# A two-layer decoder trunk on one core: three float32r products for the attention scores, factors moved to ScalarE, weight cuts tied behind evacuations, maximum taken with the bias

## The chip, the cores and the metric

The kernel runs on one core of a Trainium2 chip. What counts is the device time of one execution in microseconds; the kernel before took 751.36 us in the median of three runs (750.59 to 751.94).

## The reference, cut to what matters

The input is 256 tokens of width 1024, all in float32. There are two layers. The first mixes tokens with a dilated attention: 16 heads of 64, each in three groups (undilated, every 4th and every 16th key), whose results are weighted by the softmax of their log-denominators. The second layer uses one causal attention whose scores get a bias from summed forget gates. Each layer ends in a SwiGLU block of inner width 2816.

```python
def dilated_mixer(h, w_in, w_out):
    proj = (h @ w_in).reshape(B, S, N_GROUPS, 3, N_HEADS, HEAD_DIM)
    ...                                  # q and k rotated, v; per group:
    o, lse = dilated_band_attention(q, k, v, dil, window // dil)
    ...
    wts = jax.nn.softmax(jnp.stack(lses, axis=0), axis=0)
    o = jnp.einsum('gbsh,gbshd->bshd', wts, jnp.stack(outs, axis=0))
    return o.reshape(B, S, ATTN_WIDTH) @ w_out

def forgetting_mixer(h, w_in, b_f, w_out):
    ...
    c = lax.cumsum(log_f, axis=1)
    s = jnp.einsum('bihd,bjhd->bhij', qi, k) * scale
    s = s + ci[..., None] - ck[:, :, None, :]
    s = jnp.where(key_pos[None, :] <= qpos[:, None], s, NEG_INF)
    p = jax.nn.softmax(s, axis=-1)
    return jnp.einsum('bhij,bjhd->bihd', p, vf)

for i in range(DEPTH):                   # h is the residual stream
    h = h + mixer(rmsnorm(h, norm[i]))
    h = h + swiglu(rmsnorm(h, ffn_norm[i]), ffn_w_gu[i], ffn_w_down[i])
return rmsnorm(h, final_norm)
```

## The kernel before

Every large product is made of three float32r matmuls. A float32 operand is cut in two by `split` (lines 71 to 82): ScalarE copies it to float32r (the high half, L74) and VectorE subtracts that from the original (the low half, L78). `mm3` (L194) then sums high by high (L197), high by low and low by high (L202). Weights come as pieces of 128 x 2048: `piece` (L85) issues two loads on SP's queue into a ring of five raw buffers and makes one cut for each; `weights` (L148) keeps two pieces ahead of the one in use and makes the cuts at once, or hands the low halves to a list or orders them behind a given instruction (`after`).

The projections of the first attention run in units (`a_units`): one for each quad of four heads (hq), group g and kind w (0 q, 1 k, 2 v), with 48 products of 256 columns for q and k. Each unit's result fills one of two PSUM banks "mm". `rotated` (L423) turns q and k on VectorE: a shuffle and a product with cosines read the bank (L433, L434), then a product with sines and a sum (L435, L436). In the fourth unit (i = 3) half of the projection is done ahead, inside the third unit, so that the factors `r_a` of the norm can be spread over the columns on the way (L563) and multiplied into cosines and sines (L569) before the rotation of the third unit reads its bank.

The scores of group 0 (`scores_a`, L450) are float32 matmuls over the 64 rows of one head: for a pair of heads and two query blocks four matmuls, of 128 and of 256 keys. `softmax_a` takes maxima (L488), exponentials (L283) and multiplies by the reciprocal of the sums: for the first pair of a quad on ScalarE (L497, not in the last quad), for the second on VectorE (L499). Transposes (L293) and products with v (L304) follow some units later; the list `due` holds what is to run after which unit.

The second attention has twelve units (`b_units`), the last nine in a loop (from L922). L939 copies q (times 0.125) and k from PSUM on ScalarE. `scores_b` makes the same float32 matmuls (L855); VectorE adds the bias (L861) and takes the negative maxima (L865), ScalarE the exponentials (L283). The scores of a quad's first pair run in the middle of the unit behind its k, those of the second at that unit's end or behind it. The low halves of the weights cut in units 3 and 5 wait in the list `behind`, and `release` lets them go behind the scan of the gates and behind the first scores' sums.

The order on each engine is made by a scheduler when the program is built: by the order in the code, with `first()` moving an instruction some 300 places ahead, and with `tc.issue_after(x)` fixing that an instruction is issued behind x. At run time each engine goes through its own queue in order.

Of the kernel before, what the change touches and what calls it, by code (L numbers as in the profile page):

```python
# [16 lines left out]
P = 128  # L17
D = 1024
S = 256
# [12 lines left out]
def trunk(ctx: ExitStack, tc: tile.TileContext, T, out):  # L32
# [38 lines left out]
    def split(pair, view, src, early=True, after=None):  # L71
        hi, lo = pair
        with first() if early else nullcontext():
            a = nc.scalar.activation(view(hi), src, AF.Copy)  # L74
# [7 lines left out]
            return a, low(after)  # L82


    def piece(key, todo=None):  # L85
# [6 lines left out]
        for c in range(2):  # L92
# [7 lines left out]
            cut = lambda after=None, raw=raw, view=view: split((wh, wl), view, raw, False, after)  # L100
# [4 lines left out]
        if key == GATED:  # L105
            cut = lambda after=None: split((wh, wl), lambda y: y[:, :, 256:], wf32, False, after)
            todo.append(cut)
# [40 lines left out]
    def weights(nm, i, after=None, ahead=AHEAD):  # L148

        upto = order.index((nm, i)) + ahead  # L150
        while state["next"] <= min(upto, len(order) - 1):
# [3 lines left out]
            for cut in cuts:  # L155
                cut(after)
# [266 lines left out]
    def rotated(o, g, w):  # L423


        if g == 0:
            q = hrow(f"qk{w}")[:, :512].rearrange("p (a b) -> p a b", a=2)
# [8 lines left out]
        nc.vector.tensor_tensor(q, q, tmp, op=ALU.add)  # L436
        return q, read

    def scores_a(quad, g, pr=None):
# [5 lines left out]
        if g == 0:  # L445

            scs = [psum("sc") for _ in range(2)]
            for qb in range(2):
                for h in range(2):
                    nc.tensor.matmul(scs[h][:, qb * P:qb * P + (qb + 1) * P], q[hr[h], pr, qb * P:(qb + 1) * P],  # L450
                                     k[hr[h], pr, :(qb + 1) * P], start=True, stop=True)
# [27 lines left out]
    def softmax_a(quad):  # L479
# [49 lines left out]
    for i, (hq, g, w) in enumerate(a_units):  # L529
# [19 lines left out]
        if w < 2:  # L549
# [4 lines left out]
            if i == 2:  # L554
                values_12(quad["v"], lead)

                wt = weights("a_in", 1)
# [12 lines left out]
            q, read = rotated(o, g, w)  # L570
            quad["fm"][g, w] = q
# [275 lines left out]
    def scores_b(hq, pr):  # L847
# [5 lines left out]
        for qb in range(2):  # L853
            for h in range(2):
                last = nc.tensor.matmul(scs[h][:, qb * P:qb * P + (qb + 1) * P], b[0][own[h], pr, qb * P:(qb + 1) * P],  # L855
                                        b[1][own[h], pr, :(qb + 1) * P], start=True, stop=True)
        for h in range(2):
            s = p_tile()
            with first():
                bias_h = b["bias", pr][:, h * 3 * P:(h + 1) * 3 * P]  # L860
                added = nc.vector.tensor_tensor(s[:, :3 * P], scs[h][:, :3 * P], bias_h, op=ALU.add)  # L861
            for qb in range(2):
                j = h * 2 + qb
                sv = s[:, qb * P:qb * P + (qb + 1) * P]
# [228 lines left out]
```

## Time and profile before

| | |
|---|---|
| Median of three runs | 751.36 us |
| The profiled execution | 752.26 us |
| Its span in the profile | 750.5 us |
| Granted TensorE clock | 0.997 |
| TensorE busy | 740.2 us |
| VectorE busy | 500.7 us |
| ScalarE busy | 373.7 us |
| GpSimd busy | 67.3 us |

The profile has one execution. Rows of groups show line, engine, operation, what is written from what, shape and count, then busy time and mean ns of one, then the idle time of the engine before them and what ended it. PE is TensorE's matmuls, PEld its weight loads, DVE VectorE, ACT ScalarE, POOL GpSimd, SP the queue that issues loads. In the timeline the first two numbers are start and length in us; neighbours of one line and operation are merged, with their count. In the chain of waits the first number is a start, the second how long that step holds the chain. Matmuls overlap, so the length of one (0.28 us for 256 columns) is more than the distance between two starts. The first attention lasts until about 250 us, the second layer's from about 450 to 555 us; the rest is SwiGLU.

### The profile page before, as it was taken

To read this page: it belongs to the slowest core of one execution; us is meant where nothing else is said; L and a number is where in the kernel's file an instruction comes from. 1 tells how busy PE (TensorE), PEld (TensorE's weight loads), DVE (VectorE), ACT (ScalarE), POOL (GpSimd) and SP (SyncE) were. 2 spreads that over 40 slices of the span, in tenths; PEclk is the share of its full clock that TensorE was granted. 3 is DMA by queue.
4 is the path that set the end of the run, shared out by engine and by line. 5 is a ranking of instruction groups with operands and counts; after the bars stand their busy time and mean duration, and the time that the engine had idled before them with its cause. 6 is when DMAs were issued, how large, how long until landed. Compare 5 with 4: busy or idle time off the path is not lost.

```text
span 750.5 us, 14329 instructions
## 1 busy us (share of the span) xinstructions
PE 740.2 (99%) x5916; PEld 680.1 (91%) x5916; DVE 500.7 (67%) x752; ACT 373.7 (50%) x617; POOL 67.3 (9%) x98
## 2 busy tenths in 40 slices
PE   9999999999999999999999999999999999999996
PEld 7998989999998789999999988989889999999995
DVE  6987978876879376554556365799867545456533
ACT  7635537437427365444445355467556444445521
POOL 0600004004004000000000004312000000000001
PEclk9999999999999999999999999999999999999998
DMA  9865544645646267656567543784537665656601
GB/s 332 302 195 170 169 142 156 210 142 169 198 133 200 88 225 242 204 179 205 181 198 250 169 129 127 268 252 155 166 95 235 217 205 179 199 193 213 210 1 56
DMA packets 39441, 138.07 MB, mean 184 GB/s; under 512 B 4528, under 2 KB 5840, under 8 KB 39376
## 3 DMA queue, kind: packets, MB, share of 16 engines
q1 hardware_dynamic: 39232, 137.01, 55.3%
q8 instruction: 46, 0.75, 0.4%
q14 instruction: 19, 0.16, 0.1%
q10 hardware_dynamic: 144, 0.15, 0.1%
HBM read 136.07 MB, written 1.07 MB: 183 GB/s over the span
## 4 chain that ended last, share of the span: by engine, by line
PE 93%; ACT 2%; DVE 2%; DMA 2%; issue 1%; SPq 0%; POOL 0%; POOLq 0%; DVEq 0%; ACTq 0%
PE ps_mm L202 32%; PE ps_mm L197 17%; PE ps_tr L202 9%; PE ps_sc L202 8%; PE ps_o L202 7%; PE ps_tr L197 5%; PE ps_sc L197 4%; PE ps_o L197 4%; PE ps_o L304 2%; PE ps_tr L293 1%; DMA otl<-in_lead 1%; PE ps_sc L450 1%; PE ps_sc L466 1%; PE ps_sc L855 1%; ACT wh L74 1%; DMA raw<-in_a_in 1%
## 5 line engine op out<-in xcount | busy, mean ns | idle before, releaser
L74 ACT ACTIVATE wh<-raw 128x1024 fp32r<-128x1024 f32 x236 | 243.0, 1054 | 247.5 <-PE ps_mm L202 85.8
L78 DVE TENSOR_TENSOR wl<-raw,wh 128x1024 fp32r<-128x1024 f32 x236 | 287.7, 1238 | 81.8 <-ACT wh L74 81.5
L197 PE MATMUL ps_mm<-xt,wh 128*128 128x256 f32 x816 | 228.2, 280 | 0.7 <-DVE qk L434 0.7
L202 PE MATMUL ps_mm<-xt,wl 128*128 128x256 f32 x816 | 226.3, 277 | 0.1
L202 PE MATMUL ps_mm<-xt,wh 128*128 128x256 f32 x816 | 226.2, 277 | 0.0
L197 PEld LDWEIGHTS ps_mm<-xt,wh 128*128 128x128 f32 x816 | 153.3, 188 | 4.4 <-issue 3.3
L202 PEld LDWEIGHTS ps_mm<-xt,wl 128*128 128x128 f32 x816 | 153.4, 188 | 0.5 <-DVE wl L78 0.5
L202 PEld LDWEIGHTS ps_mm<-xt,wh 128*128 128x128 f32 x816 | 153.7, 188 | 0.0
L202 PE MATMUL ps_tr<-xt,wl 128*128 128x256 f32 x304 | 83.9, 276 | 0.0
L202 PE MATMUL ps_tr<-xt,wh 128*128 128x256 f32 x304 | 83.9, 276 | 0.0
L197 PE MATMUL ps_tr<-xt,wh 128*128 128x256 f32 x304 | 83.7, 276 | 0.0
L692 DVE TENSOR_TENSOR sa<-ps_tr,sa 128x256 f32<-128x256 f32 x38 | 16.1, 424 | 74.1 <-PE ps_tr L202 74.0
L202 PEld LDWEIGHTS ps_tr<-xt,wl 128*128 128x128 f32 x304 | 57.1, 188 | 0.0
L202 PEld LDWEIGHTS ps_tr<-xt,wh 128*128 128x128 f32 x304 | 57.1, 188 | 0.0
L197 PEld LDWEIGHTS ps_tr<-xt,wh 128*128 128x128 f32 x304 | 56.9, 188 | 0.0
L279 POOL COPY v<-v 32x256 f32<-32x256 f32 x64 | 36.1, 563 | 180.3 <-ACT v L275 177.6
L197 PE MATMUL ps_mm<-wh,xt 128*128 128x512 f32 (+1 forms) x144 | 50.1, 348 | 0.0
L202 PE MATMUL ps_mm<-wl,xt 128*128 128x512 f32 (+1 forms) x149 | 49.3, 336 | 0.0
L202 PE MATMUL ps_mm<-wh,xt 128*128 128x512 f32 (+1 forms) x149 | 49.2, 335 | 0.0
L167 POOL TENSOR_SCALAR rs<-ssq 128x1 f32<-128x1 f32 x7 | 2.1, 307 | 425.2 <-ACT junk L176 425.2
L197 PE MATMUL ps_sc<-wh,ah 128*128 128x512 f32 x80 | 31.4, 392 | 0.0
L202 PE MATMUL ps_sc<-wl,ah 128*128 128x512 f32 (+1 forms) x82 | 31.3, 385 | 0.0
(224 smaller groups left out, 1112.9 us busy)
## 6 DMA issues: line engine op xcount, KB each, us to landing
raw<-in_gu SPq DMA_DIRECT2D x88, 512.0 KB, 4.8
raw<-in_a_in SPq DMA_DIRECT2D x68, 512.0 KB, 4.4
raw<-in_dn SPq DMA_DIRECT2D x44, 512.0 KB, 4.5
raw<-in_b_in SPq DMA_DIRECT2D x24, 512.0 KB, 5.0
raw<-in_a_out SPq DMA_DIRECT2D x8, 512.0 KB, 4.5
raw<-in_b_out SPq DMA_DIRECT2D x8, 512.0 KB, 4.9
bias<-sums SPq DMA_DIRECT2D x8, 384.0 KB, 6.3
grow<-in_norms SPq DMA_DIRECT2D x4, 512.0 KB, 5.4
```

The lines of the kernel that those rows point to most:

```text
L74: a = nc.scalar.activation(view(hi), src, AF.Copy)
L78: return nc.vector.tensor_tensor(view(lo), src, view(hi).bitcast(F32), op=ALU.subtract)
L167: nc.gpsimd.tensor_scalar(m, s, rest, None, op0=ALU.add)
L197: nc.tensor.matmul(o, sh, mh, start=start, stop=False)
L202: last = nc.tensor.matmul(o[:, u], s, m[:, u], start=False, stop=end and u.stop == n)
L279: nc.gpsimd.tensor_copy(v[1 + a % 2][n:n + 32, a // 2 * S:a // 2 * S + S], by_t[a * 32:a * 32 + 32, t, g])
L293: nc.tensor.transpose(tr[:, i * P:(i + 1) * P], b, ident)
L304: nc.tensor.matmul(o[h * HD:(h + 1) * HD], v[:, c:c + HD], w(h), start=start, stop=stop)
L450: nc.tensor.matmul(scs[h][:, qb * P:qb * P + (qb + 1) * P], q[hr[h], pr, qb * P:(qb + 1) * P], k[hr[h], pr, :(qb + 1) * P], start=True, st ...
L466: nc.tensor.matmul(sc[h][c, o:o + 64], q[hr[h], pq, qb * P + a * 32:qb * P + a * 32 + 32], k[hr[h], pq].rearrange("p (b n) -> p b n", b=2) ...
L692: nc.vector.tensor_tensor(a, u, sg, op=ALU.mult)
L855: last = nc.tensor.matmul(scs[h][:, qb * P:qb * P + (qb + 1) * P], b[0][own[h], pr, qb * P:(qb + 1) * P], b[1][own[h], pr, :(qb + 1) * P], ...
```

## The change

It has four parts.

- Scores of group 0 and of the second attention: q and k are cut into high and low halves, and each float32 matmul becomes three float32r matmuls (high by high, high by low, low by high), on the same 64 rows and with the same 128 or 256 columns. In the first attention the rotated sum now goes to a buffer "qr" (two for each of these units, from the ring of three) and `split` makes the halves. In the second, L939 writes the high half and a new VectorE instruction makes the low half straight from PSUM.
- First attention: in the first three quads the factors of the second pair are applied on ScalarE too.
- Ties: the second low half of the piece cut in unit 3 is issued behind the read of the bank in `rotated`; in the second attention's loop the cuts of weights are issued behind the previous unit's q or k (high half behind high half, low half behind low half).
- Second attention: sum with the bias and negative maximum become one VectorE instruction for each query block, which writes the negated sum; the exponential reads it with scale -1.

```diff
-    def split(pair, view, src, early=True, after=None):
+    def split(pair, view, src, early=True, after=None, hold=None):
         hi, lo = pair
         with first() if early else nullcontext():
-            a = nc.scalar.activation(view(hi), src, AF.Copy)
+            with behind_(hold and hold[0]):
+                a = nc.scalar.activation(view(hi), src, AF.Copy)
...
-            return a, low(after)
+            return a, low(after or hold and hold[1])
...
+    PRODUCTS = ((0, 0), (0, 1), (1, 0))
...
         if g == 0:
-            q = hrow(f"qk{w}")[:, :512].rearrange("p (a b) -> p a b", a=2)
+            pair = ap.tile([P, 2, 2, S], F32R, tag="h", name=f"qk{w}", bufs=4)
+            q = ap.tile([P, 2, S], F32, tag="qr", name="rc", bufs=3)
...
-        nc.vector.tensor_tensor(q, q, tmp, op=ALU.add)
+        if g == 0:
+            nc.vector.tensor_tensor(tmp, q, tmp, op=ALU.add)
+            q = pair[:, 0], pair[:, 1]
+            split(q, lambda y: y, tmp, False)
+        else:
+            nc.vector.tensor_tensor(q, q, tmp, op=ALU.add)
...
-                for h in range(2):
-                    nc.tensor.matmul(scs[h][:, qb * P:qb * P + (qb + 1) * P], q[hr[h], pr, qb * P:(qb + 1) * P],
-                                     k[hr[h], pr, :(qb + 1) * P], start=True, stop=True)
+                for i, (y, z) in enumerate(PRODUCTS):
+                    for h in range(2):
+                        nc.tensor.matmul(scs[h][:, qb * P:qb * P + (qb + 1) * P],
+                                         q[y][hr[h], pr, qb * P:(qb + 1) * P], k[z][hr[h], pr, :(qb + 1) * P],
+                                         start=i == 0, stop=i == 2)
...
-                    if pr == 0 and quad["hq"] < 3:
+                    if quad["hq"] < 3:
                         nc.scalar.activation(s, s, AF.Copy, scale=f)
...
-                wt = weights("a_in", 1)
+                second = []
+                wt = weights("a_in", 1, second)
+                second.pop(0)()
...
             q, read = rotated(o, g, w)
+            if i == 2:
+                second.pop()(read)
...
-            with first():
-                bias_h = b["bias", pr][:, h * 3 * P:(h + 1) * 3 * P]
-                added = nc.vector.tensor_tensor(s[:, :3 * P], scs[h][:, :3 * P], bias_h, op=ALU.add)
+            bias_h = b["bias", pr][:, h * 3 * P:(h + 1) * 3 * P]
             for qb in range(2):
-                j = h * 2 + qb
-                sv = s[:, qb * P:qb * P + (qb + 1) * P]
-                nc.vector.tensor_reduce(nm[:, j:j + 1], sv, axis=AX.X, op=ALU.max, negate=True)
-                exps(sv, nm, den, j)
+                j, u = h * 2 + qb, slice(qb * P, qb * P + (qb + 1) * P)
+                with first():
+                    added = nc.vector.tensor_tensor_reduce(s[:, u], scs[h][:, u], bias_h[:, u], -1.0, -NEG, ALU.add,
+                                                           ALU.min, nm[:, j:j + 1])
+                nc.scalar.activation(s[:, u], s[:, u], AF.Exp, bias=nm[:, j:j + 1], scale=-1.0,
+                                     accum_out=den[:, j:j + 1])
...
+    held = None
     for i, (hq, w) in enumerate(b_units):
...
-        wt = weights("b_in", hq * 3 + w, behind if i in (3, 5) else None)
+        wt = weights("b_in", hq * 3 + w, behind if i in (3, 5) else None, hold=held)
...
-            bq[hq][w] = ap.tile([P, 2, S], F32, tag=f"fm{w}", name=f"fb{w}", bufs=2)
+            if w == 0:
+                low = ap.tile([P, 2, 2, S], F32R, tag="h", name="fl", bufs=4)
+            ov = o.rearrange("p (a b) -> p a b", a=2)
+            qk = ap.tile([P, 2, S], F32R, tag=f"fm{w}", name=f"fb{w}", bufs=2)
+            bq[hq][w] = qk, low[:, w]
+            c = (0.125, 1.0)[w]
             with first():
-                nc.scalar.activation(bq[hq][w], o.rearrange("p (a b) -> p a b", a=2), AF.Copy, scale=(0.125, 1.0)[w])
+                held = (nc.scalar.activation(qk, ov, AF.Copy, scale=c),
+                        nc.vector.scalar_tensor_tensor(low[:, w], ov, c, qk.bitcast(F32), op0=ALU.mult,
+                                                       op1=ALU.subtract))
```

More of the change, by code (lines that the diff above doesn't have):

```diff
@@ L69, in trunk, with behind_ @@
     nc.gpsimd.memset(euler, math.e)
[L71 removed]
+    def behind_(ins):
+        return tc.issue_after(ins.ins) if ins else nullcontext()
+    def split(pair, view, src, early=True, after=None, hold=None):
         hi, lo = pair
         with first() if early else nullcontext():
[L74 removed]
+            with behind_(hold and hold[0]):
+                a = nc.scalar.activation(view(hi), src, AF.Copy)
             def low(after=None):
@@ L99, in piece @@
                 view = lambda y, c=c: y[:, c * 4:c * 4 + 4, :256]
-            cut = lambda after=None, raw=raw, view=view: split((wh, wl), view, raw, False, after)
+            cut = lambda after=None, hold=None, raw=raw, view=view: split((wh, wl), view, raw, False, after, hold)
             if todo is None:
@@ L105, in piece @@
         if key == GATED:
-            cut = lambda after=None: split((wh, wl), lambda y: y[:, :, 256:], wf32, False, after)
+            cut = lambda after=None, hold=None: split((wh, wl), lambda y: y[:, :, 256:], wf32, False, after, hold)
             todo.append(cut)
@@ L146, in trunk, with weights @@
     state = {"next": 0}
-    def weights(nm, i, after=None, ahead=AHEAD):
+    def weights(nm, i, after=None, ahead=AHEAD, hold=None):
         upto = order.index((nm, i)) + ahead
@@ L155, in weights @@
             for cut in cuts:
-                cut(after)
+                cut(after, hold)
             state["next"] += 1
@@ L853, in scores_b @@
         for qb in range(2):
-            for h in range(2):
-                last = nc.tensor.matmul(scs[h][:, qb * P:qb * P + (qb + 1) * P], b[0][own[h], pr, qb * P:(qb + 1) * P],
-                                        b[1][own[h], pr, :(qb + 1) * P], start=True, stop=True)
+            for i, (y, z) in enumerate(PRODUCTS):
+                for h in range(2):
+                    last = nc.tensor.matmul(scs[h][:, qb * P:qb * P + (qb + 1) * P],
+                                            b[0][y][own[h], pr, qb * P:(qb + 1) * P],
+                                            b[1][z][own[h], pr, :(qb + 1) * P], start=i == 0, stop=i == 2)
         for h in range(2):
             s = p_tile()
-            with first():
-                bias_h = b["bias", pr][:, h * 3 * P:(h + 1) * 3 * P]
-                added = nc.vector.tensor_tensor(s[:, :3 * P], scs[h][:, :3 * P], bias_h, op=ALU.add)
+            bias_h = b["bias", pr][:, h * 3 * P:(h + 1) * 3 * P]
             for qb in range(2):
-                j = h * 2 + qb
-                sv = s[:, qb * P:qb * P + (qb + 1) * P]
-                nc.vector.tensor_reduce(nm[:, j:j + 1], sv, axis=AX.X, op=ALU.max, negate=True)
-                exps(sv, nm, den, j)
+                j, u = h * 2 + qb, slice(qb * P, qb * P + (qb + 1) * P)
[4 more added lines that the diff above has]
+                                     accum_out=den[:, j:j + 1])
             pt[pr, h] = s
```

## The prediction, made before the result was known

> **What bounds the kernel now.** I read the page first, then the waits of TensorE, then the chain and the timelines around the two places that those waits name, then the scores themselves. From the page:
>
> ```profile
> span 750.5 us, 14329 instructions
> PE 740.2 (99%) x5916; PEld 680.1 (91%) x5916; DVE 500.7 (67%) x752; ACT 373.7 (50%) x617; POOL 67.3 (9%) x98
> ```
>
> TensorE is busy for 99% of the span, so only two things can move the end: what TensorE itself executes, and the few places where it waits. The waits of TensorE (who waited for whom: us in total, times, longest) are three, and the second is the start of the program, which the change leaves alone.
>
> ```profile
> PE ps_sc L855 <- ACT fb L939: 1.6, 1, 1.6
> PE ps_o L313 <- DVE mhalf L65: 0.9, 1, 0.9
> PE ps_mm L197 <- DVE qk L434: 0.7, 1, 0.7
> ```
>
> So there are two stalls to win, one in each attention, and work on VectorE and ScalarE that stays ahead of TensorE is free.
>
> **First stall (30.05 us), the second cut's tie.** TensorE's and VectorE's timeline:
>
> ```profile
> 25.43 0.50 PE L563 MATMUL ps_tr<-ident,rs_a 128*128 128x128 f32 x3
> ...
> 29.07 0.28 PE L202 MATMUL ps_mm<-xt,wl 128*128 128x256 f32 x1
> 30.05 0.36 PE L197 MATMUL ps_mm<-xt,wh 128*128 128x256 f32 x1 [0.71 <-DVE qk L434]
> ```
> ```profile
> 27.32 1.33 DVE L78 TENSOR_TENSOR wl<-raw,wh 128x1024 fp32r<-128x1024 f32 x1 [0.21 <-ACT wh L74]
> 28.57 0.41 DVE L569 TENSOR_TENSOR rcos<-rcos,ps_tr 128x256 f32<-128x256 f32 x1
> 28.90 0.41 DVE L569 TENSOR_TENSOR rsin<-rsin,ps_tr 128x256 f32<-128x256 f32 x1
> 29.23 0.68 DVE L434 TENSOR_TENSOR qk<-ps_mm,rcos 128x512 f32<-128x512 f32 x1
> ```
>
> Products follow each other at 0.11 us, so the gap from 29.07 to 30.05 holds 0.98 - 0.11 = 0.87 us of waiting for a PSUM bank that L434 frees at 29.91. L569 needs only the bank that L563 had written by 25.9, and stands behind a subtraction of weights (27.32, 1.33 us). That subtraction is the second of its piece, which the change issues behind L434. Without it L434 ends 28.57 - 27.32 = 1.25 us earlier, at 28.66, before 29.18: the whole 0.87 us go. The two ScalarE copies of that piece stay where they are. The subtraction now stands behind L434, at 28.7; behind it wait the rest of the rotation, the next unit's read of its bank, and on SP's queue the transfer that refills its raw buffer, about 1.3 us later, in a ring of five buffers. Nothing of POOL moves. What could be late next is that next read: each of these two units gives VectorE one new low half (0.69 us), against the 5.5 us of TensorE's work in a unit. I take -0.87.
>
> **Second stall (495.88 us), the ties behind the evacuation.** TensorE's timeline, and the chain of waits before it:
>
> ```profile
> 493.97 0.28 PE L202 MATMUL ps_mm<-xt,wl 128*128 128x256 f32 x1
> 495.88 0.38 PE L855 MATMUL ps_sc<-fb,fb 64*128 64x128 f32 x2 [1.63 <-ACT fb L939]
> ```
> ```profile
> 491.39 1.48 ACT p L283 x6
> 492.87 0.95 ACT wh L74
> 493.82 0.58 ACT p L872 x2
> 494.40 0.95 ACT wh L74
> 495.35 0.49 ACT fb L939
> ```
>
> Elsewhere a first score follows its last product by 0.21 (511.72 to 511.93, below), so 1.91 - 0.21 = 1.70 us are lost. The bank was full 24 products before 493.97, at about 491.4; the copy L939 waited behind four exponentials with their accumulator reads (x6 here), which need VectorE's maxima, and behind two weight copies L74. The change shortens this from two ends. It holds the weight copy at 494.40 behind the evacuation (-0.95). And it replaces add and two reductions per head by two fused instructions. The trace has no such instruction; the rows nearest to it:
>
> ```profile
> L861 DVE TENSOR_TENSOR p<-ps_sc,bias 128x384 f32<-128x384 f32 x16 | 8.1, 545 | 4.2 <-PE ps_sc L855 4.2
> L865 DVE TENSOR_REDUCE nm_b<-p 128x1 f32<-128x256 f32 x16 | 6.5, 406 | 0.0
> L865 DVE TENSOR_REDUCE nm_b<-p 128x1 f32<-128x128 f32 x16 | 4.3, 270 | 0.0
> L692 DVE TENSOR_TENSOR sa<-ps_tr,sa 128x256 f32<-128x256 f32 x38 | 16.1, 424 | 74.1 <-PE ps_tr L202 74.0
> L987 DVE DVE_READ_ACCUMULATOR ps_sc<-hn 128x1 f32 x1 | 0.1, 142 | 0.0
> ```
>
> Per head the old cost is 0.545 + 0.406 + 0.270 = 1.22. Lowest, the fused pair costs only its additions: 0.424 for 256 columns and, on the line through 0.545 and 0.424, 0.30 for 128, so 0.73. Highest, it also pays both reductions and two accumulator reads: 0.73 + 0.68 + 0.28 = 1.69. I take additions and reads, 1.01: over 16 heads -3.4 us of VectorE (bounds -7.8 to +7.5). Against it stand eight new low halves of q and k, at 0.69 us (L78 of 512 columns, below) +5.5 us. VectorE has 85.0 - 69.8 = 15.2 us idle in this stage (windows below). That covers the net +2, and in the sum even the worst end, 7.5 + 5.5 = 13.0, though not at every instant; without the cover those us would show on TensorE. I take the stall as gone but for 0.2 us, because the low half of k must now also be ready: -1.50. Next late are the transposes that need L872, which ended at 494.40; TensorE would reach them at 495.0.
>
> **The scores on TensorE.** One block (one pair of heads) by the chain, and its inside by the timeline asked at two instants:
>
> ```profile
> 47.02 0.23 PE ps_mm L202 x2
> 47.25 0.86 PE ps_sc L450 x8
> ```
> ```profile
> 47.18 0.38 PE L450 MATMUL ps_sc<-qk,qk 64*128 64x128 f32 x2
> 47.51 0.60 PE L450 MATMUL ps_sc<-qk,qk 64*128 64x256 f32 x4
> ```
> ```profile
> L450 PEld LDWEIGHTS ps_sc<-qk,qk 64*128 64x128 f32 x64 | 4.2, 186 | 1.1 <-issue 0.5 <-DVE rt L433 0.2
> L202 PEld LDWEIGHTS ps_mm<-xt,wh 128*128 128x128 f32 x816 | 153.7, 188 | 0.0
> ```
>
> Four float32 matmuls show as eight records, each with its own weight load, two heads side by side: four steps. From 47.18 to 47.51 are one uncovered load and two steps of 128 columns, 3 x 0.11; the other 0.86 - 0.33 = 0.53 are two steps of 256 at twice that, 0.22, and 0.09 of emptying. The change makes six steps: three of 128 and three of 256. A float32r product of 256 columns with its own load takes 0.23 / 2 = 0.115 (row x2). For 128 columns no float32r row exists. Lowest is streaming alone, 0.115 / 2 = 0.06; the nearest row is the 128-wide step here, 0.11, in which a load of 128 columns also fits; highest the two float32 passes, 0.22. I take 0.11: the load stays as long when the moving side shrinks. Block: 0.11 + 3 x 0.11 + 3 x 0.115 + 0.09 = 0.875 against 0.86, over 16 blocks +0.25 us (-2.2 at the lowest step, +5.5 at the highest). Three products thus buy nothing on TensorE. They add a wait, the second product's for k's low half: behind it stands all of TensorE's queue, and on VectorE the low half itself waits for ScalarE's copy, with the weight subtractions behind it.
>
> The Trainium skill speaks against this part: "TensorE: Matmul & The Clock Gate", section "LDWEIGHTS (loading the stationary operand)", says a load's time goes by its columns and not its rows, columns / 1.2 GHz, an estimate of 107 ns here. The trace agrees (186 ns for 64 rows, 188 for 128), and by it six loads per block would take 0.64 us where four took 0.43.
>
> **VectorE and ScalarE in the first attention.** Windows (busy us and instructions of PE, PEld, DVE, ACT, POOL) and rows:
>
> ```profile
> 30.00:240.00 210.00, 209.94 (x2141) 194.21 (x2142) 174.26 (x287) 104.97 (x175) 31.56 (x58) 1.00 0.53 174
> 470.00:555.00 85.00, 83.37 (x660) 74.27 (x659) 69.80 (x124) 49.33 (x123) 14.19 (x10) 1.00 0.57 187
> ```
> ```profile
> L497 ACT ACTIVATE p<-p,c 128x384 f32<-128x384 f32 x6 | 3.6, 607 | 0.0
> L499 DVE TENSOR_SCALAR p<-p,c 128x384 f32<-128x384 f32 x10 | 5.1, 515 | 0.0
> L78 DVE TENSOR_TENSOR wl<-xw,wh 128x512 fp32r<-128x512 f32 x4 | 2.7, 687 | 0.1
> ```
>
> Twelve factors, half of 384 columns and half of 256, leave VectorE (at most 12 x 0.515 = 6.2) and cost ScalarE at most 12 x 0.607 = 7.3; eight low halves cost VectorE 5.5 and eight high halves ScalarE, at two thirds of the 0.95 that a weight copy of twice the columns takes in the chain above, about 5. VectorE stays near 174 of 210 us, ScalarE goes to 117 of 210. The factors of a quad must be there when it is transposed, a unit and more later, and the scores read q and k two units after them. I cost it at nothing: TensorE's own 209.94 us hide it. Were that cover gone, the 4 x 0.607 = 2.4 us by which a quad's factors come later on ScalarE would show, three times. Behind them on ScalarE stand weight copies for later units.
>
> **Sum.** -0.87 - 1.50 + 0.25 = -2.1 us. The profiled execution took 752.26 (span 750.5 and 1.8 around it), which makes 750.1; the median of the runs is 0.9 lower, 751.36, which makes 749.2.
>
> **Rivals.**
>
> *The ties do not bind* (7%). The stalls stay, the scores cost +0.25: 751.6. For it speaks that an instruction can still wait for its inputs in its new place; against it, that the subtraction at 27.32 and the copy at 494.40 are just the ones tied.
>
> *The wait moves from L939 to the low halves* (15%). The second product of every block needs k's low half, 0.69 us behind the copy, on VectorE.
>
> ```profile
> 510.33 3.44 DVE L78 TENSOR_TENSOR wl<-raw,wh 128x1024 fp32r<-128x1024 f32 x2
> 511.06 0.57 ACT L939 ACTIVATE fb<-ps_mm 128x512 f32<-128x512 f32 x1
> ```
> ```profile
> 511.72 0.28 PE L202 MATMUL ps_mm<-xt,wl 128*128 128x256 f32 x1
> 511.93 0.49 PE L855 MATMUL ps_sc<-fb,fb 64*128 64x128 f32 x4
> ```
>
> Rows of VectorE, ScalarE and TensorE: here the copy ends at 511.63, 0.3 us ahead of the score, and VectorE is in two weight subtractions until 513.77. If the low half comes after both, it lands at 514.4, 2.3 us late; if after one, about 0.3 late. One such case and three of 0.2 to 0.3 add 3 us: 752.2. Against it: the tie puts just these subtractions behind the low half. It decides once VectorE is more than 0.3 us late at each block.
>
> *Narrow float32r steps at float32's rate* (14%), the slower side. At 0.22 per 128-wide step each of 16 blocks gains 3 x 0.11 more: +5.3, so 754.5. It speaks for it that every float32r product of this kernel moves 256 columns or more, so the trace can't exclude it. It outweighs the two stalls from 0.16 us per step on.
>
> *Heads one after the other* (6%). If float32r on 64 rows doesn't run two heads side by side, six more steps of 0.11 per block: +10.8, so 760. Against it: the eight records above do so in float32.
>
> *Streaming alone counts* (6%). Steps at 0.06: -2.4 more, 746.8. The Trainium skill has the rule by which this would be so: "FP8 and Floating Point Precision", section "TensorE Precision Notes", counts four passes for true float32, where here three are made. The row against it is the load of 186 ns beside every record.
>
> **How the numbers follow.** My forecast has 52%: 749.2, by itself 748.3 to 750.3. About 0.2%, 1.5 us, can be told from no change here, so the border of faster is 749.9. Faster: the forecast but for a tenth (42%) and the last rival, 48%, which I round to 49. Same: that tenth, ties that don't bind, and most of the late low halves, 29. Slower: the rest, 22. The range takes in the last rival and the narrow steps, 746.8 to 755.0, and leaves out the heads one after the other.
>
> **What would show it.** Right: TensorE's waits for L434 and for the copy of k gone; the score blocks at 0.86 to 0.89 with twelve records; no new wait over 0.3 us. Wrong: 128-wide steps of 0.22, or loads of the two heads one behind the other; a wait of TensorE's loads for the low half of k; the copy of k still behind an L74; the fused instruction over 0.6 us.

## The result, and the profile after

The changed kernel takes 749.78 us (median of 13 runs, 749.06 to 750.32); the kernel before took 751.59 us beside it (13 runs, 750.59 to 754.2). The ratio is 0.9975 with a 95% interval of 0.9967 to 0.9982: faster by 0.25%. The forecast was 749.2. Ratios leave out two executions at a lower granted clock (0.753 and 0.948), both of the kernel without the fused instruction below. The profiled execution took 749.78 us, with a span of 748.0.

In the changed kernel the cuts of the weights are L79 (high) and L83 (low), the products L202 and L207, the scores L464 and L875, the rotation's reads L441 and L442, the fused instruction L884, its exponentials L886, the factors of the second attention L891 to L894, the copy of q or k L966 and its low half L967. The page's first lines, and TensorE's waits (us in total, times, longest):

```profile
span 748.0 us, 14484 instructions
PE 739.1 (99%) x5980; PEld 682.0 (91%) x5980; DVE 498.5 (67%) x772; ACT 384.2 (51%) x637; POOL 68.9 (9%) x98
```
```profile
PE ps_o L320 <- DVE mhalf L65: 0.9, 1, 0.9
PE ps_tr L298 <- DVE p L894: 0.6, 1, 0.6
PE ps_sc L393 <- ACT wh L79: 0.4, 2, 0.2
```

The first and the third row lie in the first 17 us, the start of the program. Both stalls of before are gone, and one that was not there has come (the second row). The first place, VectorE and then TensorE:

```profile
27.20 0.40 DVE L586 TENSOR_TENSOR rcos<-rcos,ps_tr 128x256 f32<-128x256 f32 x1
27.52 0.41 DVE L586 TENSOR_TENSOR rsin<-rsin,ps_tr 128x256 f32<-128x256 f32 x1
27.85 0.68 DVE L442 TENSOR_TENSOR rc<-ps_mm,rcos 128x512 f32<-128x512 f32 x1
...
29.09 1.41 DVE L83 TENSOR_TENSOR wl<-raw,wh 128x1024 fp32r<-128x1024 f32 x1
```
```profile
29.08 0.28 PE L207 MATMUL ps_mm<-xt,wl 128*128 128x256 f32 x1
29.20 0.28 PE L202 MATMUL ps_mm<-xt,wh 128*128 128x256 f32 x1
```

The subtraction of weights stands behind the rotation's reads now. L442 ends at 28.53, and the next unit's first product (29.20) follows the last one at 0.12 us; in the kernel before the same two stood 0.98 apart. The second place, ScalarE and TensorE:

```profile
490.16 0.68 ACT L893 ACTIVATE p<-p,c_b 128x128 f32<-128x128 f32 x2
490.74 0.58 ACT L966 ACTIVATE fb<-ps_mm 128x512 fp32r<-128x512 f32 x1
491.22 2.00 ACT L79 ACTIVATE wh<-raw 128x1024 fp32r<-128x1024 f32 x2
```
```profile
492.84 0.28 PE L207 MATMUL ps_mm<-xt,wl 128*128 128x256 f32 x1
493.05 0.33 PE L875 MATMUL ps_sc<-fb,fb 64*128 64x128 f32 x2
493.21 0.28 PE L875 MATMUL ps_sc<-fl,fb 64*128 64x128 f32 x2
493.32 0.28 PE L875 MATMUL ps_sc<-fb,fl 64*128 64x128 f32 x2
493.44 0.33 PE L875 MATMUL ps_sc<-fb,fb 64*128 64x256 f32 x2
493.60 0.28 PE L875 MATMUL ps_sc<-fl,fb 64*128 64x256 f32 x2
493.72 0.28 PE L875 MATMUL ps_sc<-fb,fl 64*128 64x256 f32 x2
493.93 0.33 PE L298 MATMUL ps_tr<-ident,p 128*128 128x128 f32 x1
```

The copy of k goes ahead of two weight copies, and the first score follows its last product by 0.21. The same rows show a block from inside: six steps, two heads each, 0.88 us to the next instruction. Behind the first of each width (0.16) a step takes 0.11 to 0.12 us, with 128 columns as with 256. The new stall, in VectorE's timeline and then TensorE's:

```profile
532.27 1.23 DVE L83 TENSOR_TENSOR wl<-raw,wh 128x1024 fp32r<-128x1024 f32 x1 [0.55 <-ACT wh L79]
533.41 0.28 DVE L884 CUSTOM_DVE_ANT_0 p<-ps_sc,bias 128x128 f32<-128x128 f32 x1
...
535.37 1.22 DVE L83 TENSOR_TENSOR wl<-raw,wh 128x1024 fp32r<-128x1024 f32 x1
536.50 0.17 DVE L891 RECIPROCAL c_b<-den_b 128x4 f32<-128x4 f32 x1
536.70 0.61 DVE L894 TENSOR_SCALAR p<-p,c_b 128x256 f32<-128x256 f32 x2
```
```profile
537.11 0.59 PE L298 MATMUL ps_tr<-ident,p 128*128 128x128 f32 x2 [0.62 <-DVE p L894]
```

The last scores were done at 530.7; their maxima begin at 533.41, behind a subtraction that itself waited for ScalarE, and their factors come behind another one.

Where the difference lies, from setting the traces beside each other product by product (score blocks counted by their lengths). The stretches are those of the kernel before; the second column is the changed kernel profiled once more, the third the changed kernel with float32 scores (both below); us against before:

| stretch | changed | changed again | float32 scores |
|---|---|---|---|
| 0 to 28.5, start | +0.01 | +0.18 | +0.38 |
| 28.5 to 30.2, first stall | -0.87 | -0.87 | -0.87 |
| 30.2 to 46.9, pace of the products | -0.71 | -0.71 | -0.71 |
| 46.9 to 479 (score blocks in it) | +0.37 (+0.23) | +0.27 (+0.22) | +0.04 (0) |
| 479 to 503, second stall (blocks) | -1.59 (+0.11) | -1.59 (+0.11) | -1.62 (0) |
| 503 to 534 (blocks) | -0.17 (+0.11) | -0.17 (+0.11) | +0.03 (0) |
| 534 to 545, last transposes | +0.77 | +0.75 | -0.15 |
| 545 to the end | -0.29 | 0.00 | -0.29 |
| sum | -2.48 | -2.14 | -3.19 |

Of the -0.71, 0.08 still belong to the stall: behind it the second product came at 0.20 us (30.05 to 30.25) and not at 0.11. There is one trace of the kernel before, of an execution 0.67 us above that kernel's median. So the sums are larger than the difference of the medians, 1.81.

### The profile page after: what moved, and what is told of

Same layout as the page of the kernel before. It is cut to its first block, busy times and chain, and to the rows that moved or that the text cites. A ratio compares the mean times of both kernels' runs of the same rounds, so it can differ in the third digit from the quotient of the medians.

```text
span 748.0 us, 14484 instructions
## 1 busy us (share of the span) xinstructions
PE 739.1 (99%) x5980; PEld 682.0 (91%) x5980; DVE 498.5 (67%) x772; ACT 384.2 (51%) x637; POOL 68.9 (9%) x98
## 4 chain that ended last, share of the span: by engine, by line
PE 94%; DVE 2%; ACT 2%; DMA 1%; issue 1%; SPq 0%; POOL 0%; POOLq 0%; DVEq 0%; ACTq 0%
PE ps_mm L207 33%; PE ps_mm L202 17%; PE ps_tr L207 9%; PE ps_sc L207 8%; PE ps_o L207 7%; PE ps_tr L202 5%; PE ps_sc L202 4%; PE ps_o L202 4%; PE ps_o L311 2%; PE ps_tr L298 1%; DMA otl<-in_lead 1%; PE ps_sc L464 1%; PE ps_sc L481 1%; PE ps_sc L875 1%; PE ps_tr L195 1%; ACT wh L79 1%
## 5 line engine op out<-in xcount | busy, mean ns | idle before, releaser
L79 ACT ACTIVATE wh<-raw 128x1024 fp32r<-128x1024 f32 x236 | 242.0, 1054 | 225.5 <-PE ps_tr L207 68.7
L83 DVE TENSOR_TENSOR wl<-raw,wh 128x1024 fp32r<-128x1024 f32 x236 | 287.9, 1239 | 86.2 <-ACT wh L79 86.0
L202 PE MATMUL ps_mm<-xt,wh 128*128 128x256 f32 x816 | 227.8, 280 | 0.0
L207 PE MATMUL ps_mm<-xt,wl 128*128 128x256 f32 x816 | 226.0, 277 | 0.1
L207 PE MATMUL ps_mm<-xt,wh 128*128 128x256 f32 x816 | 225.9, 277 | 0.0
L202 PEld LDWEIGHTS ps_mm<-xt,wh 128*128 128x128 f32 x816 | 153.3, 188 | 1.7 <-issue 0.3
L207 PEld LDWEIGHTS ps_mm<-xt,wl 128*128 128x128 f32 x816 | 153.4, 188 | 0.5 <-DVE wl L83 0.5
L207 PEld LDWEIGHTS ps_mm<-xt,wh 128*128 128x128 f32 x816 | 153.4, 188 | 0.0
L207 PE MATMUL ps_tr<-xt,wl 128*128 128x256 f32 x304 | 83.9, 276 | 0.0
L207 PE MATMUL ps_tr<-xt,wh 128*128 128x256 f32 x304 | 83.8, 276 | 0.0
L202 PE MATMUL ps_tr<-xt,wh 128*128 128x256 f32 x304 | 83.6, 276 | 0.0
L207 PEld LDWEIGHTS ps_tr<-xt,wh 128*128 128x128 f32 x304 | 57.1, 188 | 0.0
L207 PEld LDWEIGHTS ps_tr<-xt,wl 128*128 128x128 f32 x304 | 57.1, 188 | 0.0
L202 PEld LDWEIGHTS ps_tr<-xt,wh 128*128 128x128 f32 x304 | 56.9, 188 | 0.0
L202 PE MATMUL ps_mm<-wh,xt 128*128 128x512 f32 (+1 forms) x144 | 50.1, 348 | 0.0
L207 PE MATMUL ps_mm<-wh,xt 128*128 128x512 f32 (+1 forms) x149 | 49.2, 336 | 0.0
L207 PE MATMUL ps_mm<-wl,xt 128*128 128x512 f32 (+1 forms) x149 | 49.2, 335 | 0.0
L202 PE MATMUL ps_sc<-wh,ah 128*128 128x512 f32 x80 | 31.4, 392 | 0.0
L207 PE MATMUL ps_sc<-wl,ah 128*128 128x512 f32 (+1 forms) x82 | 31.3, 385 | 0.0
```

The lines of the kernel that those rows point to most:

```text
L83: return nc.vector.tensor_tensor(view(lo), src, view(hi).bitcast(F32), op=ALU.subtract)
L202: nc.tensor.matmul(o, sh, mh, start=start, stop=False)
L207: last = nc.tensor.matmul(o[:, u], s, m[:, u], start=False, stop=end and u.stop == n)
```

## The experiments

The experiments were made in three groups of four, and each group has its own runs of the kernel before: 751.42 us beside the ties alone, the float32 scores, the products alone and the changed kernel again; 751.17 beside the copies' half of the tie, float32 scores without that tie, the halved steps and the second timing without the fused instruction; 751.56 beside the others. So times of different groups are compared by their ratios to it.

### The ties alone

```diff
-                wt = weights("a_in", 1)
+                second = []
+                wt = weights("a_in", 1, second)
+                second.pop(0)()
...
+            if i == 2:
+                second.pop()(read)
...
-        wt = weights("b_in", hq * 3 + w, behind if i in (3, 5) else None)
+        wt = weights("b_in", hq * 3 + w, behind if i in (3, 5) else None, hold=held)
...
+                held = nc.scalar.activation(bq[hq][w], o.rearrange("p (a b) -> p a b", a=2), AF.Copy, scale=(0.125, 1.0)[w]), None
```

There are no low halves of q and k here, so in the second attention only ScalarE's weight copies are tied.

> The two ties alone on the kernel before: the second subtraction of the first pieces behind L434, and in the second attention each weight copy behind the copy of q or k. Theory A (the gain is the two stalls): the stall at 30.05 us gone (-0.87), of the 1.70 us before 495.88 the held copy's 0.95 gone, scores unchanged: -1.8 us, about 749.6 from 751.4, so as fast as the changed kernel or a little faster. Theory B (the gain needs the three products or the fused maximum): the stalls remain or are replaced by others, within 0.5 us of before, 751.0 to 751.9.

Measured: 749.47 us, ratio 0.998 (0.9972 to 0.9989). Both stalls are gone from its trace (the first -0.87 us; at the second place the score is 0.21 us behind its product again); TensorE's only new wait of note is 0.3 us, at the last quad's transposes:

```profile
PE ps_o L298 <- ACT p L881: 0.3, 1, 0.3
```

Theory A holds: the ties alone give the whole gain. The second stall goes entirely, though, and not only the 0.95 us that the expectation gave it.

### Float32 scores in the changed kernel

```diff
-            pair = ap.tile([P, 2, 2, S], F32R, tag="h", name=f"qk{w}", bufs=4)
-            q = ap.tile([P, 2, S], F32, tag="qr", name="rc", bufs=3)
+            q = hrow(f"qk{w}")[:, :512].rearrange("p (a b) -> p a b", a=2)
...
-                held = (nc.scalar.activation(qk, ov, AF.Copy, scale=c),
-                        nc.vector.scalar_tensor_tensor(low[:, w], ov, c, qk.bitcast(F32), op0=ALU.mult,
-                                                       op1=ALU.subtract))
+                held = nc.scalar.activation(qk, ov, AF.Copy, scale=c), None
```

(and in both attentions the scores as one float32 matmul for each head and query block)

> The changed kernel with the scores of both attentions back in float32 (one copy of q and k, no low halves); the ties, the fused maximum and the factors stay. Theory A: each of 16 score blocks goes from 0.885 back to 0.856 us, -0.44 us, and VectorE is rid of eight low halves in front of the transposes that now wait 0.6 us (537.1 us): 749.0 to 749.4, 0.4 to 0.8 us faster than the changed kernel. Theory C (three products pay for themselves somewhere): slower than the changed kernel by 0.5 us or more, 750.3 and over.

Measured: 748.84 us (748.2 to 749.13), ratio 0.9964 (0.9951 to 0.9978), against 749.70 (749.17 to 750.12) for the changed kernel on the same chip: the fastest kernel of this study, by 0.86 us. Its blocks take 0.856 again, and behind the start TensorE waits for nothing in its trace. Theory A holds, a little below its range, and C falls: the three products cost time. One thing more differs: without low halves the subtractions of weights are tied to nothing. That part alone is undone further down (the copies' half of that tie); its trace keeps the 0.6 us at the transposes, so this wait comes of the low halves and not of the tie. Its time, 749.37 us in another group, lies between the two, so how much of the 0.86 is the products' alone is known from the traces only: 0.45 in the blocks and about 0.9 at the transposes, with shifts elsewhere the other way.

### The products alone

The changed `rotated`, `scores_a`, the products of `scores_b` and the low halves of q and k on the kernel before; no tie, no fused instruction, factors as before.

```diff
+                for i, (y, z) in enumerate(PRODUCTS):
...
+                held = (nc.scalar.activation(qk, ov, AF.Copy, scale=c),
+                        nc.vector.scalar_tensor_tensor(low[:, w], ov, c, qk.bitcast(F32), op0=ALU.mult,
+                                                       op1=ALU.subtract))
```

> The three products alone on the kernel before: no ties, add and two reductions as before, factors as before. Theory A: both stalls stay, every block pays 0.03 us (+0.44), and without the hold the low half of k comes 0.3 us or more behind the copy at some of the eight blocks of the second attention: 751.8 to 754. Theory C: the products bring the gain, 749.8 to 750.5.

Measured: 758.0 us, ratio 1.0086 (1.0073 to 1.0098): slower by 6.6 us, far over the 0.4 to 2.6 expected. The waits of TensorE:

```profile
PE ps_sc L871 <- ACT fb L962: 2.5, 1, 2.5
PE ps_sc L871 <- DVE fl L963: 1.2, 1, 1.2
```
```profile
PE ps_tr L298 <- DVE p L890: 0.7, 1, 0.7
```

Second place: the wait for the copy of k grows from 1.6 to 2.5, and the low half adds 1.2. The rest in this place is a halved clock, shown with the run without the second tie. One thing contradicts the prediction's first step: this kernel has no first tie, and yet its trace has no first stall. ScalarE had the piece's second half 0.7 us earlier (its copy at 25.54, against 26.23 before), so the subtraction was early too.

### The changed kernel again

> The changed kernel once more, for its time beside the other three and to see what of its trace repeats: the two stalls gone, the wait of the last quad's transposes of 0.6 us back, 749.5 to 750.1. If the pace of 113 or 118 ns per product of 256 columns is set by the order of the program, the same stretches show the same pace as in the first profile; if it is chance, they differ.

Measured: 749.70 us, ratio 0.9977 (0.9968 to 0.9986). The waits repeat to 0.1 us, the 0.6 at the transposes among them. The pace nearly does: the two traces keep their distance to 0.01 us over hundreds of microseconds, and it changes in three places: by 0.17 us in the start, by 0.10 near 283 us and by 0.30 between 570 and 590 us. So most stretches show the same pace as in the first profile, and one does not.

### Without the fused instruction

```diff
-                with first():
-                    added = nc.vector.tensor_tensor_reduce(s[:, u], scs[h][:, u], bias_h[:, u], -1.0, -NEG, ALU.add,
-                                                           ALU.min, nm[:, j:j + 1])
...
+                added = nc.vector.tensor_tensor(s[:, :3 * P], scs[h][:, :3 * P], bias_h, op=ALU.add)
...
+                nc.vector.tensor_reduce(nm[:, j:j + 1], sv, axis=AX.X, op=ALU.max, negate=True)
+                exps(sv, nm, den, j)
```

> The changed kernel with one addition and two reductions per head in place of the two fused instructions. In the changed kernel's trace a head's fused pair with its accumulator reads takes 0.55 to 0.70 us where add and reductions took 1.22, so a block of two heads is done about 1.1 us later, and with it the exponentials, the copy of k behind them and its low half. Theory D (the fused maximum is what makes room for the low halves): k's low half, 0.3 us early at 493.05 now, comes up to 0.8 us late, and the transposes at 537.1 wait 0.6 to 1.7 us more: 751.0 to 752.2. Theory E (VectorE's length is covered, as the prediction's sum had it): 749.5 to 750.1.

> The changed kernel with one addition and two reductions per head once more, for its trace: by the first runs some 4.8 us slower than the changed kernel. Theory D: the wait is for k's low half in the second attention, 2 us or more at one block, and the transposes' wait at 537 grows; TensorE's waits outside the second attention are as in the changed kernel. Rival: the loss lies in many small waits of 0.1 to 0.3 us over all blocks.

Measured: ratios 1.0038 (1.0025 to 1.0051) and 1.0012 (1.0003 to 1.0022), so 2.6 to 4.6 us slower than the changed kernel, by its 0.9977. The trace of the second run:

```profile
PE ps_o L298 <- ACT p L893: 1.8, 1, 1.8
...
PE ps_sc L875 <- DVE fl L967: 0.8, 1, 0.8
```

and its window of the second attention:

```profile
470.00:555.00 85.00, 82.26 (x675) 74.18 (x674) 70.77 (x130) 50.83 (x124) 13.76 (x10) 1.00 0.56 187
```

Theory D holds in kind. The losses are few: 0.3 us at 491.7 and 1.0 us at 507.8 for a low half of k, and 1.2 us more at the last transposes. E falls: VectorE is busy for 70.8 of 85 us and yet comes late. That is only 1.0 us more than the 69.8 before, though the low halves alone take 5.5: this window holds 25 subtractions of weights at a mean of 1.24 us where the kernel before had 26 at 1.35, 4.1 us less.

Part of the loss is not VectorE's own but the clock's. In five of the seven runs that count in the first timing and four of the nine in the second a clock of 0.993 to 0.996 was granted in the mean; the changed kernel's runs have 0.997 to 0.999. One stretch of 6.8 us at half clock, as in the next experiment, would lower the mean by 0.0045 (an estimate, 3.4 of 750 us). In the second timing the four such runs have a median of 753.1 us and the five others 751.5. The profiled run is one of the five; its trace is 1.3 us longer than the changed kernel's, with 2.4 us lost in the second attention and some of it made up by a shorter start and by pace. So the clock accounts for some of the 2 us between the two timings; what is left of them stays open.

Four kernels that tie the copies order the wait at the last transposes by what VectorE has to do: 0 us with float32 scores and the fused instruction, 0.3 with float32 scores and long maxima (the ties alone), 0.6 with low halves and the fused instruction (the changed kernel), 1.8 with low halves and long maxima. Without the second attention's ties the order is another (0.7 with low halves and long maxima, the products alone; none before), so VectorE's work is not all that sets it.

### Without the second attention's tie

```diff
-        wt = weights("b_in", hq * 3 + w, behind if i in (3, 5) else None, hold=held)
+        wt = weights("b_in", hq * 3 + w, behind if i in (3, 5) else None)
```

> The changed kernel without the tie of the second attention: weight copies and weight subtractions may again go ahead of the copies and low halves of q and k. Theory A: at 493 us a weight copy of 0.95 us stands in front of the copy of k again and one or two subtractions of 1.2 us in front of its low half; with 0.3 us of margin that is a stall of 2 to 3 us, 751.5 to 753. Theory F (the shorter maxima alone cure the second stall): 749.5 to 750.3.

Measured: 756.25 us, ratio 1.0063 (1.005 to 1.0076): 6.5 us slower than the changed kernel where 2 to 3 were expected. TensorE, then VectorE, then windows (busy us and instructions of PE, PEld, DVE, ACT, POOL, the granted clock, DMA share, GB/s):

```profile
493.05 0.28 PE L207 MATMUL ps_mm<-xt,wl 128*128 128x256 f32 x1
495.45 0.33 PE L875 MATMUL ps_sc<-fb,fb 64*128 64x128 f32 x2 [2.12 <-ACT fb L966]
495.71 0.35 PE L298 MATMUL ps_tr<-ident,p 128*128 128x128 f32 x1
498.28 0.47 PE L875 MATMUL ps_sc<-fl,fb 64*128 64x128 f32 x2 [2.22 <-DVE fl L967]
498.55 0.41 PE L875 MATMUL ps_sc<-fb,fl 64*128 64x128 f32 x2
498.77 0.52 PE L875 MATMUL ps_sc<-fb,fb 64*128 64x256 f32 x2
```
```profile
491.91 5.71 DVE L83 TENSOR_TENSOR wl<-raw,wh 128x1024 fp32r<-128x1024 f32 x4
497.55 0.68 DVE L967 SCALAR_TENSOR_TENSOR fl<-ps_mm,fb 128x512 fp32r<-128x512 f32 x1
```
```profile
495.00:498.00 3.00, 0.61 (x3) 0.32 (x3) 3.00 (x3) 1.46 (x2) 0.41 (x1) 0.65 0.97 279
498.00:502.00 4.00, 3.72 (x22) 3.50 (x22) 3.51 (x12) 1.82 (x8) 0.00 (x0) 0.50 0.90 311
502.00:506.00 4.00, 4.00 (x38) 3.81 (x36) 1.64 (x5) 1.55 (x4) 0.00 (x0) 0.91 0.68 232
```

The copy of k is 2.2 us late (2.40 less the usual 0.21), and its low half, behind four subtractions in a row, 2.4 more. The clock is halved, too. The trace's record of it has half clock from 495.89 to 502.71, 6.8 us; the windows fit that (0.65 granted in the first, 0.91 in the third). It begins 0.44 us behind the end of the first wait, ahead of the second. The second wait covers its first part; from 498.28 to 502.7 steps take 0.21 to 0.32 us where they took 0.11 to 0.17, which costs about half of these 4.4 us, 2.2. A late low half at 480 adds 0.4. Less the transposes' stall, which is gone here (0.8), these make 6.4 of the 6.5. Theory A holds in kind and misses the second wait's size and the clock; F falls.

The products alone lose in the same way: there the record has half clock from 495.73 to 502.56, again 6.8 us, and the first score behind the 2.5 us wait already runs at it.

The Trainium skill, "TensorE: Matmul & The Clock Gate", section "Part 1: The HAM clock gate (the "warmup" mystery)", says that an idle window of about 3.4 us, counted freely, drops the clock to half, and that about as long of sustained work brings it back. The half agrees with the 0.50 here. The length is shorter in this case: a wait of 2.5 us had done it in the products alone and one of 2.1 us here, while waits of 1.6 us (before) and 1.8 us (without the fused instruction) had not.

### The copies' half of that tie

```diff
-                held = (nc.scalar.activation(qk, ov, AF.Copy, scale=c),
-                        nc.vector.scalar_tensor_tensor(low[:, w], ov, c, qk.bitcast(F32), op0=ALU.mult,
-                                                       op1=ALU.subtract))
+                held = nc.scalar.activation(qk, ov, AF.Copy, scale=c), None
+                nc.vector.scalar_tensor_tensor(low[:, w], ov, c, qk.bitcast(F32), op0=ALU.mult, op1=ALU.subtract)
```

> The changed kernel with half of the second attention's tie: ScalarE's weight copies stay behind the copies of q and k, VectorE's weight subtractions are free to go ahead of the low halves. Without the whole tie the low half of k stood behind four subtractions (491.91 to 497.55). Theory A (with three products it is the subtractions' half that matters): the copy of k is on time and the low half still 1.5 to 3 us late behind two or more subtractions of 1.2 us: 751.2 to 753.5. Theory J (the copies' half is enough, since a subtraction can't start before its weight copy): 749.5 to 750.1.

Measured: 749.37 us, ratio 0.9967 (0.9954 to 0.998), not to be told from the changed kernel's 0.9977. One new wait, in a block that is 0.77 us longer for it:

```profile
PE ps_sc L875 <- DVE fl L967: 0.5, 1, 0.5
```

Theory A falls, J holds but for this wait: a subtraction needs its weight copy, so holding the copies behind the copy of k holds most of the subtractions too.

### Float32 scores without that tie

The float32 kernel above with the same one line undone (`hold=held` left out).

> Float32 scores with the fused maximum, the first attention's tie and factors, but without the second attention's tie. The prediction had the stall of 1.70 us cured from two ends, 0.95 by the tie and the rest by the shorter maxima. Theory K (that split): 0.75 us or less of the stall left, 748.9 to 749.6 where with the tie it was 748.84. Theory L (without the tie two to three weight copies of 0.95 us go ahead of the copy of k, as they did in the changed kernel without it, and the shorter maxima cure nothing): a stall of 1.5 to 2.5 us, 750.3 to 751.3.

Measured: 750.12 us, ratio 0.9983 (0.9974 to 0.9992), between K's and L's times. Two waits for the copy L954:

```profile
PE ps_sc L866 <- ACT fb L954: 0.7, 2, 0.4
```

At 492.5 0.43 us of the stall are left (0.64 less 0.21), near 480 0.36 are new. So the shorter maxima alone take 1.27 of the 1.70 us at this wait. They do not keep them. A few microseconds later VectorE is late again, behind two subtractions of weights (VectorE, then TensorE):

```profile
495.22 2.47 DVE L83 TENSOR_TENSOR wl<-raw,wh 128x1024 fp32r<-128x1024 f32 x2 [1.15 <-ACT wh L79]
```
```profile
498.30 1.47 PE L866 MATMUL ps_sc<-fb,fb 64*128 64x128 f32 x8
499.70 1.82 PE L311 MATMUL ps_o<-pt,v 128*64 128x256 f32 x16
```

This block takes 1.40 us where others take 0.86, because its banks are freed late by L874, and the products with v behind it wait for VectorE's copies (L302). Together that is 0.94 us which neither the kernel before nor the float32 kernel with the tie lost. From 479 to 503 us the shorter maxima alone thus change nothing against the kernel before (+0.03); the tie alone takes the whole 1.70 (the ties alone).

### Without the first attention's tie

```diff
-                second = []
-                wt = weights("a_in", 1, second)
-                second.pop(0)()
+                wt = weights("a_in", 1)
```

> The changed kernel without the tie of the first attention's second subtraction. In the profile of the products alone, which lacks this tie, the stall at 30 us did not show: there the weight's transfer had come 0.7 us earlier and the subtraction with it. Theory A, as the prediction had it: the 0.87 us come back, 750.4 to 750.8. Theory G (the stall hangs on when the transfer lands, and the tie is worth that only in some runs): 749.7 to 750.4, and a profile with the subtraction's copy landing early has no stall.

Measured: 750.51 us, ratio 0.9985 (0.9976 to 0.9993), 0.6 us over the changed kernel by the ratios, with intervals that overlap. Its trace:

```profile
27.76 1.36 DVE L83 TENSOR_TENSOR wl<-raw,wh 128x1024 fp32r<-128x1024 f32 x1 [0.60 <-ACT wh L79]
```
```profile
29.38 0.28 PE L207 MATMUL ps_mm<-xt,wl 128*128 128x256 f32 x1
30.54 0.36 PE L202 MATMUL ps_mm<-xt,wh 128*128 128x256 f32 x1 [0.89 <-DVE rc L442]
```

The stall is back, 1.16 - 0.11 = 1.05 us: A by size. G is right as well: with the piece early (the products alone) there is none. Three traces can't say how often.

### The factors back on VectorE

```diff
-                    if quad["hq"] < 3:
+                    if pr == 0 and quad["hq"] < 3:
```

> The changed kernel with the second pairs' factors of the first attention back on VectorE. Prediction: nothing, 749.4 to 750.1, TensorE's waits as in the changed kernel. Rival: VectorE, which now also makes the low halves of q and k, comes late with one of them or with a bank's read, 0.3 us or more in each of three quads: 750.4 and over.

Measured: 749.68 us, ratio 0.998 (0.9969 to 0.9991), TensorE's waits as in the changed kernel. The factors are worth nothing.

### Narrow steps halved

```diff
-                for i, (y, z) in enumerate(PRODUCTS):
-                    for h in range(2):
...
+                for u in ((slice(0, 64), slice(64, 128)), (slice(0, 256),))[qb]:
+                    for i, (y, z) in enumerate(PRODUCTS):
+                        for h in range(2):
```

> The changed kernel with each 128-wide float32r product of the scores made as two of 64 columns, each with its own weight load: nine steps per block in place of six, the same result. Theory H (the load of 128 columns sets a narrow step, as the prediction chose): each 64-wide step takes the 0.11 us of the 128-wide one, a block 0.885 + 3 x 0.112 = 1.22 us, 16 blocks +5.4 us: 754.6 to 755.6. Theory I (the streaming of columns sets it): 0.056 us each, blocks unchanged, 749.4 to 750.2.

Measured: 753.83 us, ratio 1.003 (1.0019 to 1.004). Blocks in the chain of waits, and the loads and products of the first attention's scores (ns: least, median, most):

```profile
45.60 1.22 PE ps_sc L465 x18
```
```profile
L465 PEld LDWEIGHTS ps_sc<-qk,qk x144: 182/188/188, 45.5 to 214.3; 64*128 64x128 f32 x144
L465 PE MATMUL ps_sc<-qk,qk x144: 272/273/364, 45.5 to 214.4; 64*128 64x64 f32 x96, 64*128 64x256 f32 x48
```

A block takes 1.22 us, as H had it to the hundredth: half the columns, the same 0.11 us. Against the changed kernel's 0.9977 that is 4.0 us and not 5.4; by the traces 0.9 of the difference lies at the last transposes, whose stall is gone from this one. I falls. A fixed 0.11 us for every step, whatever it loads, is not the reason either: in the changed kernel's products with v a load has 64 columns, and steps that move 64 columns of float32 follow each other faster:

```profile
96.41 0.40 PE L311 MATMUL ps_o<-pt,v 128*64 128x64 f32 x8
```

These eight records are four steps, as two heads go side by side, and the last record lasts 0.22 us, so a step takes (0.40 - 0.22) / 3 = 0.06 us.

The Trainium skill ("TensorE: Matmul & The Clock Gate", section "LDWEIGHTS (loading the stationary operand)") counts a load by its columns, an estimate of 107 ns for these 128; the steps of 111 to 112 ns agree.

## Why the prediction was right, step by step

The time and its sign came out as forecast, by the two stalls named. That the sum fits so closely is in part luck (under "The sum"). The steps differ in how well they stood.

**First stall, -0.87.** Right to the digit at its place, and the tie is the cause where the piece lands late. That a run can be without the stall, with no tie, was not in the prediction.

**Second stall, -1.50.** -1.59 from 479 to 503, with 0.11 of blocks in it, so -1.70 of stall. The division of the cure was wrong: "shortens this from two ends" reads as a sum of 0.95 and the rest. The tie alone takes all of it. The shorter maxima alone take 1.27 at this wait, and TensorE loses as much again at others before 503 us.

**The fused pair, 1.01 us per head with 0.73 as its lowest.** Too dear. The instructions are 0.28 and 0.42 us long and follow each other at 0.21 and 0.34, with 0.08 for an accumulator's read that overlaps; a head takes about 0.55:

```profile
L884 DVE CUSTOM_DVE_ANT_0 p<-ps_sc,bias x32: 277/352/420, 481.1 to 534.2; 128x128 f32<-128x128 f32 x16, 128x256 f32<-128x256 f32 x16
L884 DVE DVE_READ_ACCUMULATOR2_ANT nm_b<- x32: 75/83/85, 481.3 to 534.5; 128x1 f32 x32
```

The lower bound was taken from other additions' durations, 0.424 and 0.30, and these fit the two lengths; but each instruction here starts about 0.07 us before the one ahead of it has ended.

**"That covers the net +2, and in the sum even the worst end."** The step that failed. An idle sum over a stage of 85 us was read as cover. With maxima as long as before, VectorE had the low halves' 5.5 us more to do, far from the 13.0 that were to be covered, and the kernel lost 2.6 to 4.6 us against the changed one, some of it by the clock; 2.4 us were lost in the second attention in the execution at full clock. It did not tell in the forecast, because the fused instruction was cheap. That instruction does not bring the gain; it pays for the low halves.

**Next late.** The prediction looked for the next wait at the transposes near 495 and expected none over 0.3 us. It was at the transposes of the last quad, +0.75, the largest delay missing from the sum.

**Scores, +0.25.** +0.45 (0.881 to 0.889 a block), with the reason chosen, the load of 128 columns, borne out by the halved steps. "Three products thus buy nothing on TensorE" holds, and with VectorE's share the kernel with them is 0.86 us slower.

**Factors at nothing.** Right.

**The sum.** -2.1 stood against -1.8 in the medians and -2.1 to -2.5 in two profiles. The missing +0.75 and +0.2 were paid by the pace of the products between 30 and 47 us, -0.63 without the stall's 0.08, which no step names. That is luck. It is not the tie's doing: without the tie, behind its own stall, the pace there is the fast one too. What sets it is not known.

**The rival of the low halves, 15% at 752.2,** is no chance but a condition. With the tie it doesn't occur; without it the kernel takes 756.3. Its price was too low: it had one low half 2.3 us late and some small ones, and the run has the copy 2.2 us late, the low half 2.4 more, and half the clock behind them.

## What to carry to other kernels

Before pricing a cheaper-looking product, ask what sets its step: here a step took 0.11 us with 64, 128 or 256 columns of float32r, beside the same load of 128 columns, so three narrow products could not undercut float32's passes. A sum of idle time on a side engine is no cover: follow its order up to each result that TensorE needs. Undo each part of a change alone, and follow the trace past the wait that it shortens: here one part took 1.3 us from a wait and TensorE lost as much at others close by, and another part only spent what a third had saved. In this kernel it was enough to tie the copies; the subtractions that read them followed, but for one wait of 0.5 us.

## What was not expected of the hardware

*Two paces of one product.* Products of 256 columns follow each other at 113 or at 118 ns, in whole stretches and at the same granted clock. Between 32 and 44 us the median is 118 ns in the kernel before and 113 in the twelve other traces with full clock in that stretch; between 160 and 195 us it is 114 before and 118 in the changed kernel. Over all steps of 115 to 125 ns the time above 113 adds up to 4.7 us before, 3.6 and 3.8 in two profiles of the changed kernel, and 2.7 to 4.3 in the others. It repeats in most stretches where the program repeats, and shifts by up to a microsecond with edits that do not touch it: as much as an edit of this size is worth. What sets it was not found.

*Half the clock after a wait of over 2 us.* A stall of TensorE of 2.5 us (the products alone) and one of 2.1 us (without the second attention's tie) were charged again: in both the granted clock was half for 6.8 us, from about 2.5 us after the last product had ended. A second wait that falls into this time, 2.2 us in the one trace and 1.2 in the other, runs while the clock is low and hides a part of it; the work behind the wait pays for the rest.
